# Attention scores in three matmuls per key block: three full ones before; two full ones and one over 32 rows after

## The chip, the cores and the metric

The kernel runs on one core of a Trainium2 chip. A core has five engines with a queue of instructions each: PE (TensorE, matrix products; its weight loads are listed apart as PEld), DVE (VectorE), ACT (ScalarE), POOL (GpSimd) and SP (SyncE, which here only issues DMAs). The engines run on their own and wait for each other through semaphores. Each takes its instructions in the order in which the build wrote them down. PE reads from SBUF and writes to PSUM; a bank of PSUM holds a tile of 128x512 float32 numbers in this kernel. The metric is the time of one execution on the device in microseconds (us), lower being better.

## What is computed

The program is one block of a transformer: modulated norms, an input projection, latent attention over 2048 tokens and 256 context tokens, a retention branch, an output projection and a convolutional feed-forward part. The change is in the scores of the attention:

```python
def softmax_attention(q, k, v):
    s = jnp.einsum('bqhd,bkhd->bhqk', q, k).astype(jnp.float32) * MLA_SCALE
    p = jax.nn.softmax(s, axis=-1).astype(v.dtype)
    return jnp.einsum('bhqk,bkhd->bqhd', p, v)
```

There are 8 heads. A query and a key have 96 features: 64 without position ("nope") and 32 rotary ones ("pe"; those of the key are the same for all heads). There are 2304 keys (2048 + 256).

## The kernel before

PE multiplies in float32r, so a float32 operand is kept as two float32r parts, high and low, whose sum is the operand. A product of two such operands is a sum of up to four products of parts.

**Tiles of the attention.** The outer loop runs over 128 pairs of a head and a tile of 128 queries (i = 0 to 127, 16 tiles for each head). The keys come in five blocks `CH`: four of 512 and one of 256. For each pair and block, `qk(i, ci)` makes the scores `sc` (128 queries x up to 512 keys) in one PSUM bank: three matmuls that add into the bank (L875), then one DVE instruction that scales them into the SBUF tile `p` and takes their maximum (L877). The operands are stacked along the 128 rows of the array. `ka` has the 64 nope features of the keys, the high part in rows 0 to 63 and the low part in rows 64 to 127. `kp` has the 32 rotary features as high, high, low, low. The query tile `q` (`q_first`, later `qp`) has three slabs: nope high twice, nope low twice, and rotary high, low, high, low. So each matmul fills all 128 rows, and the three of them make all four products of parts.

**What follows the scores.** `soft(i)` takes the maximum over the blocks and ACT makes the exponentials of a row of 2304 (L889). Two iterations later `tr` transposes `p` in pieces of 128x128 on PE (L914) into a PSUM tile `tr` (up to four pieces in a bank), ACT copies it as the high part `ph` (L67), and DVE makes the low part `pl` (L68). Then `pv` multiplies with the values (L929, L930). A retention branch (`ret_back`) runs in the same stage with little work.

**PSUM.** The stage uses eight banks: three for `sc` (pool `ats`), four for `tr` and one for `pv`.

**Order.** The attention loop calls its functions by a list of numbers for each i. The tile framework then orders the instructions of each engine itself at build time, by the program's order and by when it expects operands and buffers, so that instructions of neighbouring calls stand mixed. That order is fixed in the program. SP loads `ka` and `vv` one head ahead and `qp` one block of 512 queries ahead.

**Another place with a short matmul.** In the first stage, `columns` makes matmuls over 5 rows with 2 columns to stream (L278); `gemv` (L267) uses 4 columns of the array, and so does the transpose of the row sums in `inv` (L896).

Of the kernel before, what the change touches and what calls it, by code (L numbers as in the profile page):

```python
# [9 lines left out]
F32 = mybir.dt.float32  # L10
# [8 lines left out]
P = 128  # L19
# [3 lines left out]
KT = D // P  # L23
# [15 lines left out]
def hybrid_block(ctx: ExitStack, tc: tile.TileContext, x, xT, c, cx, c_ctx, w_ada1, b_ada1, w_ada2, b_ada2, g_norm1,  # L39
# [44 lines left out]
    def rms_inv(ms, n):  # L84
        """(ms + EPS) ** -0.5 for n columns"""
        r = small.tile([P, 8], F32, name="rstd")
        pool.tensor_scalar(out=r[:, :n], in0=ms, scalar1=EPS, scalar2=None, op0=ALU.add)
        pool.tensor_tensor(out=r[:, :n], in0=r[:, :n], in1=mhalf[:, :n], op=ALU.pow)
        return r
# [20 lines left out]
    # chunks of tokens of the FFN: first token, tokens, first of the tokens read (four more, one on each inner side at least)  # L110
# [10 lines left out]
    wmx = ExitStack()  # L121
    wmm = wmx.enter_context(tpool(name="wm", bufs=1))
    with ExitStack() as rf:
# [22 lines left out]
        def row_norm(src, xt, pl_, tag):  # L146
            """a token tile and the inverse of its norm"""
# [8 lines left out]
        def prep_norm(ti, pl_, tag):  # L156
            """a token tile with the features on the partitions, and the inverses of the tokens' norms in every partition"""
# [11 lines left out]
        def prep(ti):  # L169
            """normed, modulated and split"""  # L170
# [15 lines left out]
        def kv_state(first, kvs):  # L186
            """states before the first chunk, forward and backward"""
# [22 lines left out]
        # modulation of the first stage and projections of the context, by blocks of 256 features  # L210
        with tpool(name="ada", bufs=1) as ap_, tpool(name="adap", bufs=1, space=PSUM) as pp:
# [8 lines left out]
            # columns: high and low part for c, the same for c_ctx; unsplit beside zeros  # L220
# [32 lines left out]
            def gemv(b, q):  # L253
                """a quarter of the products of c and c_ctx with the weights of a block"""
# [15 lines left out]
            def columns(b):  # L270
                """shift and scale of a block, features on the partitions"""
# [91 lines left out]
        def mod_units(mp):  # L363
            """modulation of the later stages: gt1, sh2, sc2, gt2"""
# [145 lines left out]
    # 4 KB slots, shared by the raw weights of the last stages  # L510
# [16 lines left out]
    kp = kq.tile([P, NK], F32R, name="kp")  # L527
# [3 lines left out]
    def load_k(ka, h, b):  # L531
        o, n = BLK[b]
        for a in range(2):
            dma(ka[64 * a:64 * a + 64, o:o + n], kn_d[a][b][h * 64:(h + 1) * 64, :])

    def load_kp(b):
        o, n = BLK[b]
        dma(kp[:, o:o + n], kp_d[b])

    def load_q(q, h, b):  # L540
        for a in range(2):
            for r in range(2):
                dma(q[64 * r:64 * r + 64, a, :], qn_d[a][b][h * 64:(h + 1) * 64, :])
        for r in range(4):
            dma(q[32 * r:32 * r + 32, 2, :], qp_d[r % 2][b][h * 32:(h + 1) * 32, :])

# [1 line left out]
    with tpool(name="mpw", bufs=1) as wmp, tpool(name="mp", bufs=2) as wk, \  # L548
# [32 lines left out]
        def front(ti):  # L581
            """latents and rotary key of one token tile"""
# [192 lines left out]
    with tpool(name="at", bufs=2) as wk, \  # L775
            tpool(name="atp", bufs=1, space=PSUM) as pp, tpool(name="ats", bufs=3, space=PSUM) as pps:
# [15 lines left out]
        def ret_back(ti):  # L792
# [3 lines left out]
            cp = pp.tile([P, 512], F32, name="tr", bufs=4)  # L796
# [21 lines left out]
            ps = pp.tile([P, 512], F32, name="tr", bufs=4)  # L818
# [44 lines left out]
        def qk(i, ci):  # L863
# [9 lines left out]
            sc = pps.tile([P, 512], F32, name="sc")  # L873
            for a in range(3):
                pe.matmul(sc[:, 0:cn], lhsT=q[:, a, qs], rhs=(ka if a < 2 else kp)[:, c0:c0 + cn],  # L875
                          start=(a == 0), stop=(a == 2))
# [14 lines left out]
        def inv(h, b):  # L891
            """1 / row sums of a block of queries, as a row on 64 partitions"""
            rs = state.pop(("rs", h, b))
            dve.reciprocal(rs, rs)
            ps = pp.tile([P, 512], F32, name="tr", bufs=4)
# [8 lines left out]
        def tr(i, ci):  # L904
# [7 lines left out]
            ps = pp.tile([P, 512], F32, name="tr", bufs=4)  # L912
# [38 lines left out]
        def first_wo(i, k):  # L951
            """a part of the output projection's first tile, between the last products of the attention"""
# [5 lines left out]
        for i in range(NI + 3):  # L958
# [8 lines left out]
            if i >= 3 and j < NI // 2:  # L967
                if i % 2:
                    todo += [(3.7, pv, j, 0), (4.7, pv, j, 1)]
                else:  # L970
                    todo += [(0.7, pv, j, 2), (1.7, pv, j, 3), (2.7, pv, j, 4)]
# [27 lines left out]
            if i == NI - 1:  # L999
                split_wo(0, (w1, "ka1"), pool)  # L1000
                split_wo(1, (w1, "p"), pool)
                oT1 = kq.tile([P, 2, KT, P], F32R, name="oT1", tag="kp")
# [13 lines left out]
    def up_raw(f, tiles=None):  # L1016
        """weights of a pair of tiles of up-projected features (linear part, gated part), in halves of the rows"""
# [12 lines left out]
    # The up projection of a pair of tiles [2 x 128 features] x [2 x 512 rows] and of a chunk [2 x 512 rows] x  # L1030
    # [2 halves of the tokens] goes by Strassen's and Winograd's seven products of halves.
    # Operands from weights: A (linear; rows 1, 2), G (gated; rows 1, 2)
    #   S1 = G1 + G2, S2 = S1 - A1, S3 = A1 - G1, S4 = A2 - S2
    # operands from tokens: X, Y (rows 1; halves 1, 2), V, W (rows 2; halves 1, 2)
    #   T1 = Y - X, T2 = W - T1, T3 = W - Y, T4 = V - T2
    # linear: A1 X + A2 V | A1 X + S2 T2 + S1 T1 + S4 W
    # gated: A1 X + S2 T2 + S3 T3 + G2 T4 | A1 X + S2 T2 + S3 T3 + S1 T1
    WHOME = {"A1": 0, "S1": 0, "S2": 0, "S3": 0, "A2": 1, "G2": 1, "S4": 1}

    def up_w(f, *ks, home=None):  # L1040
        """operands from weights"""
# [19 lines left out]
    def up_sums(c_, k, va, vb):  # L1061
        """sums of the operands from the tokens of a chunk, for a pair of blocks of rows, in two places of memory"""
# [482 lines left out]
```

## Time and profile before

| | |
|---|---|
| median of 3 runs | 3487.3 us (3483.93 to 3490.97) |
| span of the profiled execution | 3483.1 us |
| busy in the span | PE 3301.2 us (95%), PEld 2938.8 (84%), DVE 2816.8 (81%), ACT 1657.4 (48%), POOL 1705.5 (49%) |
| attention stage, 762 to 1714 us of the span | PE 943.89 of 952 us, DVE 792.89, ACT 661.24 |
| mean granted TensorE clock | 0.984 of full speed |

How to read it: a PE row is a group of matmuls; its busy time runs from the start of the first to the modelled end of the last, and since matmuls overlap at their ends, the distance from start to start (the step) tells more than the duration. A PEld row is a weight load, which normally goes on under the matmul before it. "idle" in brackets is how long the engine stood still before the row, with what released it; "issue" means that nothing which the profile shows was waited for. The form "128*128" gives the rows and columns of the array that an instruction uses, "5*128" means 5 rows.

### The profile page before, as it was taken

What the parts mean: (1) busy time and instruction counts of PE and PEld (TensorE: products, weight loads), DVE (VectorE), ACT (ScalarE), POOL (GpSimd) and SP (SyncE); (2) the same over time, 40 slices, a digit from 0 to 9 for tenths busy, and PEclk for the clock granted to TensorE, in tenths of its full rate; (3) what the DMA queues carried; (4) which work ended last, traced back from release to release, by engine and by line L of the source; (5) the groups of instructions that cost most, each with busy time, mean ns of one, the idle gap of its engine ahead of it and who ended that gap; (6) DMA issues with size and microseconds to landing.
All of it is one profiled execution on the core that took longest, in us unless ns stands there. A gap on an engine that the chain in (4) does not pass through costs nothing. (4 is left out here: it accounts for less than half of the span.)

```text
span 3483.1 us, 53186 instructions
## 1 busy us (share of the span) xinstructions
PE 3301.2 (95%) x19262; PEld 2938.8 (84%) x19262; DVE 2816.8 (81%) x4969; ACT 1657.4 (48%) x2791; POOL 1705.5 (49%) x1440
## 2 busy tenths in 40 slices
PE   7999999999999999999999998998899998899998
PEld 4888889888999999999987887887788887788887
DVE  4666654457888888888765899999999999999998
ACT  4333334336676766776632343444444444333333
POOL 2322223222111111111144899888788887777774
PEclk9999999999999999999999999999999999999999
DMA  7444435773232232221146434223322223321212
GB/s 267 151 154 146 146 111 191 237 248 103 82 95 80 83 89 89 59 77 56 48 145 185 144 119 141 73 73 123 124 80 82 76 73 121 121 67 61 67 61 79
DMA packets 233822, 394.26 MB, mean 113 GB/s; under 512 B 29508, under 2 KB 106948, under 8 KB 233304
## 3 DMA queue, kind: packets, MB, share of 16 engines
q1 hardware_dynamic: 184640, 334.86, 30.3%
q10 hardware_dynamic: 48920, 56.01, 4.8%
q8 instruction: 152, 2.49, 0.3%
q14 instruction: 110, 0.90, 0.1%
HBM read 293.76 MB, written 97.01 MB: 112 GB/s over the span
## 5 line engine op out<-in xcount | busy, mean ns | idle before, releaser
L68 DVE TENSOR_TENSOR pl<-tr,ph 128x512 fp32r<-128x512 f32 (+1 forms) x640 | 389.1, 629 | 85.5 <-ACT ph L67 85.1
L877 DVE TENSOR_SCALAR_CACHE_REDUCE p<-sc 128x512 f32<-128x512 f32 (+1 forms) x640 | 393.0, 628 | 62.2 <-PE sc L875 50.7
L1151 PE MATMUL u<-T,wS 128*128 128x322 f32 (+1 forms) x2376 | 418.3, 323 | 8.2 <-DVE ua L1296 4.7
L67 ACT CAST ph<-tr 128x512 fp32r<-128x512 f32 (+1 forms) x640 | 329.8, 544 | 198.4 <-PE tr L914 190.5
L1151 PEld LDWEIGHTS u<-T,wS 128*128 128x128 f32 x2376 | 392.1, 191 | 27.3 <-issue 5.0
L71 PE MATMUL d<-dw,z 128*128 128x512 f32 x704 | 297.0, 422 | 113.6 <-DVE acc L1373 112.3
L875 PE MATMUL sc<-ka,qp 128*128 128x512 f32 (+1 forms) x1120 | 346.7, 391 | 0.0
L914 PE MATMUL tr<-ident,p 128*128 128x128 f32 x2304 | 343.3, 273 | 0.0
L889 ACT ACTIVATE p<-p,nb 128x2304 f32<-128x2304 f32 x128 | 284.8, 2225 | 64.3 <-DVE nb L884 60.7
L929 PE MATMUL pv<-ph,vv 128*128 128x256 f32 x1152 | 312.5, 297 | 0.0
L914 PEld LDWEIGHTS tr<-ident,p 128*128 128x128 f32 x2304 | 275.7, 140 | 33.8
L930 PE MATMUL pv<-pl,vv 128*128 128x256 f32 x1152 | 292.5, 286 | 0.0
L73 PE MATMUL d<-dw,z 128*128 128x512 f32 x704 | 283.5, 403 | 2.2 <-DVE z L68 2.2
L72 PE MATMUL d<-dw,z 128*128 128x512 f32 x704 | 284.3, 404 | 0.0
L71 PEld LDWEIGHTS d<-dw,z 128*128 128x128 f32 x704 | 135.2, 192 | 160.5 <-DVE acc L1373 139.1
L945 POOL TENSOR_TENSOR oT<-oT,rB 64x512 f32<-64x512 f32 x32 | 41.1, 1285 | 460.3 <-DVE oT L940 455.4
L68 POOL TENSOR_TENSOR wA<-ust,wA 128x512 fp32r<-128x512 f32 x130 | 208.5, 1604 | 82.9 <-ACT wA L67 82.8
L1373 DVE TENSOR_TENSOR acc<-acc,d 128x512 f32<-128x512 f32 x352 | 235.8, 677 | 15.3 <-PE d L73 13.3
L1353 POOL TENSOR_TENSOR dst<-dst,gt 128x512 f32<-128x512 f32 x132 | 237.8, 1815 | 14.4 <-DMA dst<-in_w_down_dram 11.8
L68 POOL TENSOR_TENSOR wS<-ust,wS 128x512 fp32r<-128x512 f32 x130 | 207.3, 1611 | 70.3 <-ACT wS L67 70.3
L68 POOL TENSOR_TENSOR wS<-s,wS 128x512 fp32r<-128x512 f32 x132 | 234.8, 1778 | 7.0 <-ACT wS L67 6.9
L875 PE MATMUL sc<-kp,qp 128*128 128x512 f32 x620 | 232.6, 375 | 0.0
(371 smaller groups left out, 8726.3 us busy)
## 6 DMA issues: line engine op xcount, KB each, us to landing
ust<-in_w_up_dram SPq DMA_DIRECT2D x132, 512.0 KB
dst<-in_w_down_dram SPq DMA_DIRECT2D x132, 256.0 KB
xt<-in_x_dram SPq DMA_DIRECT2D x32, 512.0 KB
wtg<-in_w_ada_dram SPq DMA_DIRECT2D x64, 256.0 KB
qp<-qn_d SPq DMA_DIRECT2D x124, 128.0 KB
v_d<-vt SPq DMA_DIRECT2D x18, 512.0 KB
wt<-in_w_ada_dram SPq DMA_DIRECT2D x16, 512.0 KB
xc<-in_xT_dram SPq DMA_DIRECT2D x16, 512.0 KB
```

What stands on the lines that cost most here:

```text
L67: act.copy(hi, src)
L68: (eng or dve).tensor_tensor(out=lo, in0=src, in1=f32(hi), op=ALU.subtract)
L71: pe.matmul(ps, lhsT=l[0], rhs=r[0], start=first, stop=False)
L72: pe.matmul(ps, lhsT=l[0], rhs=r[1], start=False, stop=False)
L73: pe.matmul(ps, lhsT=l[1], rhs=r[0], start=False, stop=last)
L875: pe.matmul(sc[:, 0:cn], lhsT=q[:, a, qs], rhs=(ka if a < 2 else kp)[:, c0:c0 + cn], start=(a == 0), stop=(a == 2))
L877: dve.tensor_scalar(out=p[:, c0:c0 + cn], in0=sc[:, 0:cn], scalar1=SCALE, scalar2=None, op0=ALU.mult, op1=ALU.max, accum_out=mx[:, ci:ci + 1])
L889: act.activation(p, p, AF.Exp, bias=nb, accum_out=state["rs", h, b][:, k:k + 1])
L914: pe.transpose(ps[:, k * P:(k + 1) * P], p[:, (k0 + k) * P:(k0 + k + 1) * P], ident)
L929: pe.matmul(o[:, 0:256], lhsT=vv[:, kk, :], rhs=ph[:, k, :], start=(kk == 0), stop=False)
L930: pe.matmul(o[:, 0:256], lhsT=vv[:, kk, :], rhs=pl[:, k, :], start=False, stop=(kk == NKT - 1))
L1151: pe.matmul(ps[:, 0:nh], lhsT=w[:, a, k, :], rhs=t[b][:, k, :], start=(k == 0 and a == b), stop=(k == HK - 1 and a == 1))
```

## The change

The three matmuls of a block are arranged anew. The first stays (nope high against key nope high and low). The second now holds, along its 128 rows, nope low against key nope high (rows 0 to 63), rotary high against key rotary high (64 to 95) and rotary high against key rotary low (96 to 127), in a new operand `kb`, of which there are two, one for even and one for odd heads. What is left, rotary low against key rotary high, is a matmul over 32 rows only: key block c lies in rows 32c to 32c + 31 of a new tile `kr`, and the third slab of the query tile has rotary low four times, once for each quarter of the rows. In the program text the 32-row matmuls of blocks 0 to 3 stand together ahead of the others, each into its own bank. The products of a low part with a low part are left out. PSUM is shared out as four banks for `sc` and three for `tr`. Three lines that time `pv` within an iteration, and the tag of a later buffer, change too.

```diff
-    kp = kq.tile([P, NK], F32R, name="kp")
+    kb = [kq.tile([P, NK], F32R, name=f"kb{a}") for a in range(2)]
+    kr = kq.tile([P, 768], F32R, name="kr")
...
         for a in range(2):
             dma(ka[64 * a:64 * a + 64, o:o + n], kn_d[a][b][h * 64:(h + 1) * 64, :])
+        dma(kb[h % 2][0:64, o:o + n], kn_d[0][b][h * 64:(h + 1) * 64, :])
...
-        dma(kp[:, o:o + n], kp_d[b])
+        for t in kb:
+            dma(t[64:96, o:o + n], kp_d[b][0:32, :])
+            dma(t[96:128, o:o + n], kp_d[b][64:96, :])
+        c, r = divmod(b, 4)
+        dma(kr[32 * r:32 * r + 32, 512 * c:512 * c + n], kp_d[b][0:32, :])
...
-        for a in range(2):
-            for r in range(2):
-                dma(q[64 * r:64 * r + 64, a, :], qn_d[a][b][h * 64:(h + 1) * 64, :])
+        for r in range(2):
+            dma(q[64 * r:64 * r + 64, 0, :], qn_d[0][b][h * 64:(h + 1) * 64, :])
+            dma(q[64 + 32 * r:96 + 32 * r, 1, :], qp_d[0][b][h * 32:(h + 1) * 32, :])
+        dma(q[0:64, 1, :], qn_d[1][b][h * 64:(h + 1) * 64, :])
         for r in range(4):
-            dma(q[32 * r:32 * r + 32, 2, :], qp_d[r % 2][b][h * 32:(h + 1) * 32, :])
+            dma(q[32 * r:32 * r + 32, 2, :], qp_d[1][b][h * 32:(h + 1) * 32, :])
...
-            tpool(name="atp", bufs=1, space=PSUM) as pp, tpool(name="ats", bufs=3, space=PSUM) as pps:
+            tpool(name="atp", bufs=1, space=PSUM) as pp, tpool(name="ats", bufs=4, space=PSUM) as pps:
...
-            cp = pp.tile([P, 512], F32, name="tr", bufs=4)
+            cp = pp.tile([P, 512], F32, name="tr", bufs=3)
...
-            sc = pps.tile([P, 512], F32, name="sc")
-            for a in range(3):
-                pe.matmul(sc[:, 0:cn], lhsT=q[:, a, qs], rhs=(ka if a < 2 else kp)[:, c0:c0 + cn],
-                          start=(a == 0), stop=(a == 2))
+            if ci in (0, 4):
+                for c in range(ci, min(ci + 4, 5)):
+                    rs, n = slice(32 * (c % 4), 32 * (c % 4) + 32), CH[c][1]
+                    state["sc", c] = pps.tile([P, 512], F32, name="sc")
+                    pe.matmul(state["sc", c][:, 0:n], lhsT=q[rs, 2, qs], rhs=kr[rs, 512 * (c // 4):512 * (c // 4) + n],
+                              start=True, stop=False)
+            sc = state.pop(("sc", ci))
+            for a in range(2):
+                pe.matmul(sc[:, 0:cn], lhsT=q[:, a, qs], rhs=(ka, kb[h % 2])[a][:, c0:c0 + cn], start=False, stop=(a == 1))
...
-                    todo += [(3.7, pv, j, 0), (4.7, pv, j, 1)]
+                    todo += [(2.7, pv, j, 0), (4.7, pv, j, 1)]
                 else:
-                    todo += [(0.7, pv, j, 2), (1.7, pv, j, 3), (2.7, pv, j, 4)]
+                    todo += [(0.7, pv, j, 2), (2.7, pv, j, 3), (4.7, pv, j, 4)]
...
-                oT1 = kq.tile([P, 2, KT, P], F32R, name="oT1", tag="kp")
+                oT1 = kq.tile([P, 2, KT, P], F32R, name="oT1", tag="kb0")
```

The build's order on PE, at two places. First, PE's first rows of the attention before the change; the numbers in the names tell buffers apart, so that one `sc` number is one key block.

```order
L875 MATMUL sc_7419<-ka_first_4835,q_first_4836 128x512 x2
L875 MATMUL sc_7419<-kp_4834,q_first_4836 128x512
L875 MATMUL sc_7424<-ka_first_4835,q_first_4836 128x512 x2
L875 MATMUL sc_7424<-kp_4834,q_first_4836 128x512
L875 MATMUL sc_7429<-ka_first_4835,q_first_4836 128x512 x2
L875 MATMUL sc_7429<-kp_4834,q_first_4836 128x512
```

The same place in the changed kernel; `kr` marks the matmuls over 32 rows (L886).

```order
L886 MATMUL sc_7447<-kr_4836,q_first_4838 128x512
L886 MATMUL sc_7449<-kr_4836,q_first_4838 128x512
L886 MATMUL sc_7451<-kr_4836,q_first_4838 128x512
L886 MATMUL sc_7453<-kr_4836,q_first_4838 128x512
L890 MATMUL sc_7447<-ka_first_4837,q_first_4838 128x512
L890 MATMUL sc_7447<-kb0_4834,q_first_4838 128x512
L890 MATMUL sc_7449<-ka_first_4837,q_first_4838 128x512
```

For the first tile of queries the four 32-row matmuls stand together, ahead of the full ones. Second, PE in the middle of the attention before the change (within head 5).

```order
L875 MATMUL sc_16041<-ka1_15206,qp_15615 128x512 x2
L875 MATMUL sc_16041<-kp_4834,qp_15615 128x512
L875 MATMUL sc_16053<-ka1_15206,qp_15615 128x512 x2
L875 MATMUL sc_16053<-kp_4834,qp_15615 128x512
L914 MATMUL tr_16046<-ident_63,p_15823 128x128 x4
L875 MATMUL sc_16065<-ka1_15206,qp_15615 128x512 x2
L875 MATMUL sc_16065<-kp_4834,qp_15615 128x512
```

A like place of the changed kernel, also within head 5; `pv` rows there belong to the tiles before.

```order
L886 MATMUL sc_15459<-kr_4836,qp_15295 128x256
L890 MATMUL sc_15459<-ka1_15273,qp_15295 128x256
L890 MATMUL sc_15459<-kb1_4835,qp_15295 128x256
L943 MATMUL pv_15345<-ph_15220,vv0_13664 128x256
L886 MATMUL sc_15495<-kr_4836,qp_15295 128x512
L890 MATMUL sc_15495<-ka1_15273,qp_15295 128x512
L890 MATMUL sc_15495<-kb1_4835,qp_15295 128x512
L886 MATMUL sc_15497<-kr_4836,qp_15295 128x512
L890 MATMUL sc_15497<-ka1_15273,qp_15295 128x512
L890 MATMUL sc_15497<-kb1_4835,qp_15295 128x512
```

Here each 32-row matmul stands alone, right ahead of the two full ones of its own block. In PE's whole order the four stand together once, at the first tile; the other 636 of the 640 stand alone, each with full matmuls or transposes on both sides.

## Rows read from the trace of the kernel before

**Rows 1.** Busy us (and instructions) of PE, PEld, DVE, ACT, POOL; clock; DMA.
```profile
762.00:1714.00 952.00, 943.89 (x6652) 863.16 (x6652) 792.89 (x2320) 661.24 (x1035) 168.45 (x140) 0.99 0.28 82
```

**Rows 2.** Waits of PE in the attention: us in total, times, longest.
```profile
PE sc L875 <- DVE p L877: 8.1, 1, 8.1
```

**Rows 3.** Groups of instructions in the attention: busy us, mean ns, idle before.
```profile
L877 DVE TENSOR_SCALAR_CACHE_REDUCE p<-sc 128x512 f32<-128x512 f32 x511 | 342.1, 682 | 52.9 <-PE sc L875 42.3 <-PE tr L914 6.3
...
L68 DVE TENSOR_TENSOR pl<-tr,ph 128x512 fp32r<-128x512 f32 x503 | 336.5, 683 | 81.7 <-ACT ph L67 81.4
...
L889 ACT ACTIVATE p<-p,nb 128x2304 f32<-128x2304 f32 x127 | 282.5, 2225 | 64.3 <-DVE nb L884 60.7 <-DVE pl L68 1.5 <-DVE p L877 1.0
L67 ACT CAST ph<-tr 128x512 fp32r<-128x512 f32 x504 | 281.5, 586 | 155.0 <-PE tr L914 147.5 <-DVE pl L68 6.2
```

**Rows 4.** Timeline of PE on one key block: start us, us, engine, line.
```profile
1506.41 0.39 PE L875 MATMUL sc<-kp,qp 128*128 128x512 f32 x1
...
1506.64 0.63 PE L875 MATMUL sc<-ka,qp 128*128 128x512 f32 x2
...
1507.10 0.39 PE L875 MATMUL sc<-kp,qp 128*128 128x512 f32 x1
```

**Rows 5.** Timeline where PE goes from full matmuls to 5-row ones.
```profile
32.56 0.57 ACT L275 COPY rows<-pr 4x512 f32<-4x512 f32 x1
...
36.69 0.19 PEld L73 LDWEIGHTS po<-wr,hx 128*128 128x128 f32 x1
...
36.92 0.39 PE L73 MATMUL po<-wr,hx 128*128 128x512 f32 x1
...
37.24 0.18 PEld L278 LDWEIGHTS tr<-rcol,rows 5*128 5x128 f32 x1 [0.36 <-issue]
37.24 0.27 PE L278 MATMUL tr<-rcol,rows 5*128 5x2 f32 x1
```

**Rows 6.** Timeline where PE goes from transposes to 5-row matmuls.
```profile
23.30 0.66 PE L238 MATMUL tr<-ident,xc 128*128 128x128 f32 x4
...
23.89 0.29 PEld L278 LDWEIGHTS tr<-rcol,rows 5*128 5x128 f32 x2 [0.17 <-issue]
```

**Rows 7.** Timeline where PE goes back from 5-row matmuls to full ones.
```profile
54.37 0.61 ACT L67 CAST hx<-hf 128x512 fp32r<-128x512 f32 x1
...
54.52 1.05 PE L278 MATMUL tr<-rcol,rows 5*128 5x2 f32 x8 [1.12 <-ACT rows L275]
...
55.49 0.19 PEld L71 LDWEIGHTS po<-wr,hx 128*128 128x128 f32 x1
55.49 0.50 PE L71 MATMUL po<-wr,hx 128*128 128x512 f32 x1
55.83 0.40 PE L72 MATMUL po<-wr,hx 128*128 128x512 f32 x1
```

**Rows 8.** Timeline where PE uses 4 columns between full matmuls.
```profile
35.05 0.39 PE L72 MATMUL po<-wr,hx 128*128 128x512 f32 x1
...
35.28 0.63 PE L267 MATMUL pr<-wt,s 128*4 128x512 f32 x2
...
35.75 0.40 PE L73 MATMUL po<-wr,hx 128*128 128x512 f32 x1
...
1498.03 0.28 PE L930 MATMUL pv<-pl,vv 128*128 128x256 f32 x1
...
1498.05 0.08 PEld L896 LDWEIGHTS tr<-ident,rs 128*4 128x4 f32 x1
...
1498.15 0.19 PEld L929 LDWEIGHTS pv<-ph,vv 128*128 128x128 f32 x1
```

**Rows 9.** Timeline of SP: a query block's nope loads as they are issued.
```profile
1509.45 2.38 SPq L58 DMA_DIRECT2D qp<-qn_d x4
```

More of the change, by code (lines that the diff above doesn't have):

```diff
@@ L817, in ret_back @@
             yield
-            ps = pp.tile([P, 512], F32, name="tr", bufs=4)
+            ps = pp.tile([P, 512], F32, name="tr", bufs=3)
             for h in range(RH):
@@ L894, in inv @@
             dve.reciprocal(rs, rs)
-            ps = pp.tile([P, 512], F32, name="tr", bufs=4)
+            ps = pp.tile([P, 512], F32, name="tr", bufs=3)
             pe.transpose(ps[0:QN, 0:P], rs, ident)
@@ L911, in tr @@
             p = state["p", i]
-            ps = pp.tile([P, 512], F32, name="tr", bufs=4)
+            ps = pp.tile([P, 512], F32, name="tr", bufs=3)
             for k in range(kn):
```

## The prediction

> **What bounds the kernel now.** I began with the busy times by stretches. In the attention stage PE is busy 943.89 of 952.00 us at a granted clock of 0.99, while DVE has 792.89 us of work and ACT 661.24 [rows 1]. The 8.1 us that PE lacks are one single wait [rows 2]; everywhere else in the stage its next instruction could start. So the stage lasts as long as PE's work: 952 / 128 = 7.44 us for each tile of 128 queries. DVE's idle time there is time in which it waits for PE's scores or for ACT's copy of the transposes [rows 3], so DVE is the next bound, 17% below PE. What the change is worth is therefore read from the steps of PE. In a key block, matmuls over 128 rows and 512 columns follow each other every 0.23 us: 1506.41, 1506.64, and after two of them 1507.10 [rows 4]. Each lasts 0.39 us, so a matmul's end lies 0.39 - 0.23 = 0.16 us after the last of its columns went in.
>
> **The change part by part.**
>
> *The matmuls themselves.* Before, a block of 512 keys takes three steps of 0.23 us. After, it takes two full matmuls and one over 32 rows that streams the same 512 columns. Only if the four 32-row matmuls run side by side do their columns cost less. For that they have to stand next to each other in PE's order, and by the order that the build wrote down they do so once, at the first tile. The other 636 stand alone, each ahead of the two full matmuls of its own block. The reason can be read from the order too: a 32-row matmul opens a bank, the banks of `sc` come free one at a time as DVE empties them, and when one comes free PE is given that block whole. So the columns saved are those of one tile, 3 x 0.23 = 0.7 us in all, which I neglect. Columns cost as much as before.
>
> *Going to 32 rows and back.* This is the term that decides. No row of before has a float32r matmul over 32 rows. The nearest ones are the float32 matmuls over 5 rows in the first stage, of which I take the three places where nothing else was waited for.
> On the way in: a weight load normally starts with the matmul before it, as that of L73 does at 36.69 [rows 5]. L73 itself starts at 36.92, and its columns are through one step later, at 37.15. The load for five rows starts only at 37.24, 0.09 us after that, with PEld idle for no cause that the profile shows; its data had been copied since 33.13 (32.56 + 0.57) [rows 5]. The two-column matmul ends at 37.51; less the 0.16 us, its columns go in at 37.35. That is 0.43 us after those of L73, where a step is 0.23: 0.20 us lost. After transposes it is alike: the four end at 23.96, and the load of the five-row matmuls starts at 23.89 after 0.17 us of idle time put down to issue [rows 6].
> On the way out: the eight five-row matmuls end at 55.57 (54.52 + 1.05), so the columns of the last go in at about 55.41, and being two they need next to no time. The load for L71 starts at 55.49, though its operand was cast by 54.98; L71 ends at 55.99, so its columns go in at 55.99 - 0.39 = 55.60 [rows 7]. That is 0.19 us lost; the next matmul comes one step on, its end at 56.23.
> So a visit to 32 rows would cost 0.20 + 0.19 = 0.39 us, for 512 and for 256 columns alike, since it is made of the end of one matmul and the load for the next. There are 636 + 1 = 637 visits: 637 x 0.39 = 248 us.
> Bounds of this term: below, nothing. Float32r matmuls that use 4 columns of the array come and go without a gap: 35.05, 35.28, two steps, 35.75; a transpose with 4 columns between `pv` matmuls has its load at once as well, at 1498.05 and 1498.15 [rows 8]. These change columns, not rows. If only the late start of the load counts and the load itself is hidden, 0.09 us twice: 115 us. I take the 5-row rows, since they are the only ones that change the number of rows, and they show the gap each time.
> The Trainium skill, page "TensorEngine Tiling (Array Packing)", section Tiling Modes (Key Properties), says that going from one tiling mode to another drains TensorE, and counts 128x32 as a mode like 32x128. The five-row rows agree (0.09 us from the last column to the next load); the 4-column rows do not, and there the measurement decides. By the page every visit drains twice, and the time is the one of the sum below; by rows of the 4-column kind none does, and it is that of the first rival.
>
> *Banks.* Four for `sc` instead of three, three for `tr` instead of four. A bank of `tr` is held from the transposes through ACT's copy (0.59 us) and DVE's subtraction (0.68), and up to one exponential of 2.23 us on ACT and some DVE work may lie ahead [rows 3]: some 2 to 4.5 us. Three banks come round every 3/5 of a tile, 4.5 us at the old pace and 3/5 x (7.44 + 5 x 0.39) = 5.6 at the new one. With the lost time in place this is covered; without it, a few tenths of a microsecond in a tile may show. I take nothing, with an upper bound of 0.3 us a tile, 38 us. DVE and ACT work as before and have more room, not less: 6.2 and 5.2 us in 9.4.
>
> *Loads.* `kb` adds 5 loads for each of 8 heads, `kp` becomes 20 more, a query block has 9 for 8 (32 more): 92, at 2.38 / 4 = 0.6 us each on SP 55 us of issuing [rows 9], spread over the attention and the stage before it. `kb` of a head is loaded during the head before, and the queue stands idle more than it works; DMA is busy 28% there [rows 1]. What it costs if that cover is gone: the last block's loads before the first tile, 5 x 0.6 = 3 us, once. I take nothing.
>
> **The sum.** 3483.1 us (span) + 248 = 3731 us. The median of the runs is 4.2 us above the span, so 3735 us is what I expect of it. The attention stage would go from 952 to 1200 us, 9.4 us a tile; the stages before and after keep their order (after the attention, eight lines of PE's order differ) and so their times.
>
> **The rivals.**
> *Float32r over 32 rows comes and goes without a gap.* The 4-column rows speak for it: there a change of shape costs nothing [rows 8]. Against it: those keep all rows. Then PE's steps are as before, and the time is 3487 us, up to 3525 if three banks for `tr` show.
> *Half the price:* the load is hidden behind the gap (115 us, 3602), or only one of the two ways costs (0.2 x 637 = 127 us, 3615).
> *The four run side by side after all* and the kernel is faster. Per tile the full three matmuls over 4.5 blocks are 13.5 steps, 3.1 us; two full ones are 9 steps, and the quarters one of 512 and one of 256 columns, 1.5 steps: 3 steps less, 0.69 us, 88 us in all, 3399 us. DVE would allow it: 793 us of work in 864. It is decided by the order alone: it needs the four next to each other in most tiles, and they are so in one of 128. I can see only a PE that overlaps a 32-row matmul with neighbours that fill all rows, for which no row speaks.
> The Trainium skill, page "TensorE: Matmul & The Clock Gate", Part 3, gives 3.07 times for four 32-row matmuls of 512 columns in different row groups; at that figure (an estimate) four would take 4 x 0.23 / 3.07 = 0.30 us. No row here shows four together.
>
> **How the numbers follow.** Full price 0.74, half price 0.10, no gap 0.12, side by side 0.03, more than 38 us above the sum 0.01. The predicted time is that of the full price; its own range is 3700 to 3775 (0.34 to 0.39 us a visit, and the banks' 38 us). The range for 8 in 10 takes in the half price: 3595 to 3775. A measurement of this kernel can tell about 0.2%, 7 us, from no change. Faster: side by side, and 0.02 of the no-gap case, 0.05. Same: 0.07 of the no-gap case. Slower: the rest, 0.88.
>
> **What would show it.** In the profile after: weight loads of L886 that start some 0.32 us after the full matmul ahead of them instead of with it, and those of the first L890 likewise after the 32-row matmul; each block some 1.08 us of PE instead of 0.69 us; 9.4 us a tile; DVE waiting for `sc` more than before; no wait of PE for DVE beyond single ones. If L886's loads start with the matmul ahead, the main term is wrong. If PE's waits for `tr` or `sc` banks grow, the bank term is; and if the granted clock of the stage falls below 0.99 with PE no longer full, a cost that I left out has come in.

## The result and the profile after

The changed kernel takes 3769.9 us (median of 4 runs, 3758.59 to 3783.52) against 3485.7 us in the same series: 1.0815 times, 95% interval 1.0789 to 1.0841. It is slower by 284 us, and the time lies in the predicted range, 35 us above its point. The span of its profiled execution is 3769.6 us.

Nearly all of it came in the attention. From its first `sc` matmul to its last `pv` matmul it took 973.3 us before (762.4 to 1735.7) and 1252.6 us after (764.9 to 2017.4), 279 us more; the stage ahead is 2.4 us longer and the rest 4.8 us. The windows (busy us and instructions of PE, PEld, DVE, ACT, POOL; clock; DMA) show it in the time span of [rows 1], in a stretch of its middle and in one near its end.

```profile
762.00:1714.00 952.00, 942.93 (x5205) 687.64 (x5206) 627.40 (x1839) 514.99 (x816) 146.36 (x128) 0.99 0.26 77
1000.00:1200.00 200.00, 198.57 (x1117) 145.39 (x1115) 131.90 (x385) 109.80 (x172) 24.70 (x23) 1.00 0.21 64
1800.00:2000.00 200.00, 194.86 (x1014) 141.28 (x1013) 120.30 (x337) 101.00 (x155) 18.22 (x10) 0.94 0.11 33
```

Against [rows 1], PE is as busy as before (942.93 of 952 us) but gets through 5205 matmuls in place of 6652. DVE and ACT fall with it, so neither is the bound. PE is slower at its own work, which a busy time can't show; its steps can. The timelines of PE and of its weight loads on two key blocks of the same tile:

```profile
1508.79 0.50 PE L886 MATMUL sc<-kr,qp 32*128 32x512 f32 x1
1509.22 0.50 PE L890 MATMUL sc<-ka,qp 128*128 128x512 f32 x1
1509.55 0.40 PE L890 MATMUL sc<-kb,qp 128*128 128x512 f32 x1
1509.88 0.50 PE L886 MATMUL sc<-kr,qp 32*128 32x512 f32 x1
...
1509.22 0.19 PEld L890 LDWEIGHTS sc<-ka,qp 128*128 128x128 f32 x1 [0.24 <-issue]
1509.32 0.19 PEld L890 LDWEIGHTS sc<-kb,qp 128*128 128x128 f32 x1
1509.88 0.18 PEld L886 LDWEIGHTS sc<-kr,qp 32*128 32x128 f32 x1 [0.37 <-issue]
```

A block takes 1.09 us (1508.79 to 1509.88) where [rows 4] has 0.69. The load for the 32-row matmul starts at 1509.88, 0.33 us after the full matmul of 1509.55, and the load for the next full one only 0.43 us after the 32-row matmul; the load of `kb`, between two full matmuls, starts at 1509.32, with 0.23 us to go. These are the two gaps of [rows 5] and [rows 7], in float32r and at 32 rows.

Two things are new. The waits of PE in the attention (us in total, times, longest) hold short waits for `sc` in 29 places, where [rows 2] had a single one of 8.1 us, which is gone:

```profile
PE sc L886 <- DVE p L891: 12.3, 29, 0.8
PE tr L928 <- DVE pl L68: 1.9, 4, 0.6
```

And the granted clock falls to the lower of its two levels, 1.2 GHz, for 47.8 us of the stage in five stretches (before: 10.2 us in one). The first begins at 1302.9. The timeline of PE there has a wait for a bank, lone 32-row matmuls, and then a full matmul of 0.79 us for 0.50:

```profile
1299.43 0.38 PE L928 MATMUL tr<-ident,p 128*128 128x128 f32 x2
1300.61 0.38 PE L886 MATMUL sc<-kr,qp 32*128 32x256 f32 x1 [0.79 <-DVE p L891]
...
1301.35 0.49 PE L886 MATMUL sc<-kr,qp 32*128 32x512 f32 x1
...
1302.43 0.49 PE L886 MATMUL sc<-kr,qp 32*128 32x512 f32 x1
1302.85 0.79 PE L890 MATMUL sc<-ka,qp 128*128 128x512 f32 x1
```

**PE's steps, added up.** For every two neighbouring matmuls of the stage I took the distance between their ends, less what such a matmul takes in an unbroken row (0.233 us for 512 columns, 0.119 for 256, 0.109 for a transpose), and added these excesses by kind. They sum to 288.7 us after and 10.5 before; the difference, 278, is the stage's 279 but for 1 us (8.7 of the 10.5 before are the one long wait of [rows 2]). At full clock 624 steps into 32 rows lose 134.3 us and 622 out of them 122.5; the rest is 27 such steps at the lower clock (12.5 us) and 19 us of other steps, most of them transposes and at the lower clock too. At 0.39 us the 637 visits are 248 us of the difference; some 30 us more are to be explained.

### The profile page after: what moved, and what is told of

It is laid out like the page before. It is cut to its first block, busy times and chain, and to the rows that moved or that the text cites. A ratio compares the mean times of both kernels' runs of the same rounds, so it can differ in the third digit from the quotient of the medians.

```text
span 3769.6 us, 53343 instructions
## 1 busy us (share of the span) xinstructions
PE 3575.0 (95%) x19262; PEld 2959.3 (79%) x19262; DVE 2831.6 (75%) x4969; ACT 1653.9 (44%) x2791; POOL 1705.9 (45%) x1440
## 4 chain that ended last, share of the span: by engine, by line
PE 60%; DVE 23%; issue 6%; POOL 4%; DMA 4%; ACT 2%; SPq 0%; DVEq 0%; ACTq 0%; POOLq 0%
PE sc L890 11%; PE sc L886 7%; PE tr L928 7%; PE u L1165 6%; PE pv L943 4%; PE pv L944 4%; PE pj L71 3%; PE pj L72 3%; PE pj L73 3%; DVE s L1067 2%; DVE acc L1387 2%; DVE ya L1287 2%; DVE th L1349 2%; PE d L71 2%; DVE z L68 1%
## 5 line engine op out<-in xcount | busy, mean ns | idle before, releaser
L891 DVE TENSOR_SCALAR_CACHE_REDUCE p<-sc 128x512 f32<-128x512 f32 (+1 forms) x640 | 377.7, 631 | 111.5 <-PE tr L928 105.7
L944 PE MATMUL pv<-pl,vv 128*128 128x256 f32 x1152 | 316.1, 305 | 0.3 <-DVE pl L68 0.3
L886 PE MATMUL sc<-kr,qp 32*128 32x512 f32 x620 | 295.4, 476 | 12.0 <-DVE p L891 12.0
L943 PE MATMUL pv<-ph,vv 128*128 128x256 f32 x1152 | 303.9, 289 | 0.0
L890 PE MATMUL sc<-ka,qp 128*128 128x512 f32 (+1 forms) x560 | 271.3, 485 | 0.0
```

Of the source, the lines that this page charges most:

```text
L886: pe.matmul(state["sc", c][:, 0:n], lhsT=q[rs, 2, qs], rhs=kr[rs, 512 * (c // 4):512 * (c // 4) + n], start=True, stop=False)
L890: pe.matmul(sc[:, 0:cn], lhsT=q[:, a, qs], rhs=(ka, kb[h % 2])[a][:, c0:c0 + cn], start=False, stop=(a == 1))
L891: dve.tensor_scalar(out=p[:, c0:c0 + cn], in0=sc[:, 0:cn], scalar1=SCALE, scalar2=None, op0=ALU.mult, op1=ALU.max, accum_out=mx[:, ci:ci + 1])
L943: pe.matmul(o[:, 0:256], lhsT=vv[:, kk, :], rhs=ph[:, k, :], start=(kk == 0), stop=False)
L944: pe.matmul(o[:, 0:256], lhsT=vv[:, kk, :], rhs=pl[:, k, :], start=False, stop=(kk == NKT - 1))
```

## The experiments

Two theories. **Visits:** each visit of PE to 32 rows has one price, 0.39 us. **Banks, order, loads:** the loss, or part of it, comes from four banks for `sc` and three for `tr` in place of three and four, from the rotary matmuls written ahead of their blocks, or from the new loads. All runs compute what the changed kernel computes; those that read more rows than hold data have zeros in the others. The table gathers them; "four ahead" means that the program text has the rotary matmuls of blocks 0 to 3 ahead of the others, as in the changed kernel; "stage" is from the first `sc` matmul to the last `pv` matmul of the profiled execution.

| run | visits | banks sc/tr | median us | ratio to before, 95% | stage us |
|---|---|---|---|---|---|
| before | 0 | 3/4 | 3484.6 to 3487.1 | 1 | 973.3 |
| e9 | 0 | 3/4 | 3493.2 | 1.0019 (1.0010 to 1.0028) | 979.6 |
| e8 | 256 | 3/4 | 3585.0 | 1.0287 (1.0271 to 1.0303) | 1071.3 |
| e2 | 640 | 3/4 | 3736.4 | 1.0712 (1.0689 to 1.0735) | 1222.2 |
| e10 (64 rows) | 640 | 3/4 | 3729.5 | 1.0697 (1.0682 to 1.0712) | 1212.1 |
| e11 | 0 | 3/3 | 3570.6 | 1.0248 (1.0231 to 1.0266) | 1061.9 |
| e5 | 0 | 4/3 | 3583.9 | 1.0284 (1.0267 to 1.0301) | 1072.2 |
| e1 (four ahead) | 0 | 4/3 | 3587.2 | 1.0290 (1.0273 to 1.0308) | 1074.4 |
| e4 (four ahead) | 256 | 4/3 | 3642.6 | 1.0450 (1.0434 to 1.0465) | 1127.4 |
| after (four ahead) | 637 | 4/3 | 3769.9 | 1.0815 (1.0789 to 1.0841) | 1252.6 |
| e12 | 640 | 4/3 | 3773.5 | 1.0823 (1.0801 to 1.0844) | 1279.4 |
| e3 (four together) | 128 | 4 as one/3 | 3879.7 | 1.1132 (1.1114 to 1.1149) | 1371.7 |
| e6 (four together) | 128 | 4/3 | 3581.9 | 1.0279 (1.0263 to 1.0294) | 1073.2 |
| e7 (three together) | 128 | 3/4 | 3528.4 | 1.0125 (1.0109 to 1.0140) | 1016.3 |

### e1: all rows

```diff
-    kr = kq.tile([P, 768], F32R, name="kr")
+    kr = kq.tile([P, NK], F32R, name="kr")
+    pool.memset(f32(kr), 0.0)
...
-                    pe.matmul(state["sc", c][:, 0:n], lhsT=q[rs, 2, qs], rhs=kr[rs, 512 * (c // 4):512 * (c // 4) + n],
+                    pe.matmul(state["sc", c][:, 0:n], lhsT=q[:, 2, qs], rhs=kr[:, CH[c][0]:CH[c][0] + n],
```

> The changed kernel with one thing undone: the matmul over the rotary keys reads all 128 rows, with zeros under its 32 rows, so its numbers are the same and it never goes to 32 rows; the order of the program's code and the banks (four for the scores, three for the transposes) stay as changed. If the visits to 32 rows are the loss (0.39 us each, 637 of them, 248 us), the time falls from 3770 to 3485 to 3525 us: 3770 less 248 is 3522, and less if the waits and the stretches at the lower clock go with the visits. If the banks, the order of the code or the four-fold loads of queries are the loss, it stays above 3700 us.

Measured: 3587.2 us, what neither theory gave. The visits are gone and 183 us with them, but 100 us are left, with PE waiting for banks (lines at e5).

### e2: visits with the banks of before

```diff
-            tpool(name="atp", bufs=1, space=PSUM) as pp, tpool(name="ats", bufs=4, space=PSUM) as pps:
+            tpool(name="atp", bufs=1, space=PSUM) as pp, tpool(name="ats", bufs=3, space=PSUM) as pps:
...
-            cp = pp.tile([P, 512], F32, name="tr", bufs=3)
+            cp = pp.tile([P, 512], F32, name="tr", bufs=4)
...
+            r, g = ci % 4, 512 * (ci // 4)
+            sc = pps.tile([P, 512], F32, name="sc")
+            pe.matmul(sc[:, 0:cn], lhsT=q[32 * r:32 * r + 32, 2, qs], rhs=kr[32 * r:32 * r + 32, g:g + cn],
+                      start=True, stop=False)
```

> The changed kernel with its 32-row matmuls kept, but each is written with its own block again, and the scores have three banks and the transposes four, as before the change. If the visits to 32 rows are the loss, it stays at 3735 to 3775 us (3735 if the waits for banks and the lower clock came from the banks, 3770 if they come from the visits). If banks and order are the loss, it falls to 3500 us or less.

Measured: 3736.4 us. In its windows PE is full and the clock is whole, so nothing but PE's own steps is left:

```profile
1000.00:1200.00 200.00, 200.00 (x1128) 148.83 (x1126) 139.39 (x396) 112.50 (x177) 24.77 (x24) 1.00 0.22 63
1800.00:1980.00 180.00, 180.00 (x1015) 134.74 (x1015) 120.39 (x324) 102.46 (x156) 23.08 (x12) 1.00 0.13 36
```

Its steps at full clock: 626 into 32 rows lose 0.192 us each on average, 619 out into a score matmul 0.197. That is 0.39 us a visit, the price of the prediction.

### e4: two blocks of five

```diff
+                    rs = slice(32 * c, 32 * c + 32) if c in (0, 2) else slice(0, P)
...
-                    pe.matmul(state["sc", c][:, 0:n], lhsT=q[rs, 2, qs], rhs=kr[rs, 512 * (c // 4):512 * (c // 4) + n],
+                    pe.matmul(state["sc", c][:, 0:n], lhsT=q[rs, 2, qs], rhs=kr[rs, CH[c][0]:CH[c][0] + n],
```

> As the run with full rows, but blocks 0 and 2 of each query tile go to 32 rows and blocks 1, 3 and 4 read all 128 rows with zeros: 256 visits in place of 637. If each visit has its price (0.39 us), the time is that of the run with full rows plus 100 us, 3585 to 3625 us. If the price is by tile, paid once however many visits a tile has, it stays within 30 us of the changed kernel's 3770 us.

Measured: 3642.6 us, 55 us above e1 and outside both expectations. Its steps say why: the visits lose 102 us at full clock (253 in, 0.207 each, and 254 out, 0.196), but the losses of the other `sc` and `tr` steps, 39.0 and 60.6 us in e1, are 23.6 and 26.6 here. A PE that visits comes later to the banks, and waits less for them.

### e3: four together in one tile of four banks

```diff
+            if ci == 0:
+                state["sc"] = pps.tile([P, 4, 512], F32, name="sc")
+                for c in range(4):
+                    rs = slice(32 * c, 32 * c + 32)
+                    pe.matmul(state["sc"][:, c, :], lhsT=q[rs, 2, qs], rhs=kr[rs, :], start=True, stop=False)
+            if ci < 4:
+                sc = state["sc"][:, ci, :]
+            else:
+                sc = pp.tile([P, 512], F32, name="tr", bufs=3)
+                pe.matmul(sc[:, 0:cn], lhsT=q[:, 2, qs], rhs=k4, start=True, stop=False)
```

> The four 32-row matmuls of blocks 0 to 3 are made to stand together at every query tile: the four blocks' scores are one tile of four banks, so that all four become ready at once; block 4's rotary part reads all 128 rows with zeros, into a bank of the transposes. If a visit has one price and the four run side by side, a tile takes 0.30 us less on PE than before the change (four rotary parts at 0.93 us become one at 0.24 and one visit at 0.39): 128 times 0.30 is 38 us, 3448 us, unless the one four-bank tile makes PE wait for the evictions, which could cost up to 1 us per tile (3490 to 3600 us) with PE waiting at the 32-row matmuls' line for DVE. If the four don't run side by side, 0.70 us per tile more: 3537 us with no such wait in the trace.

Measured: 3879.7 us, the slowest of all and above every expectation, although the four stand together at all 128 tiles and run side by side. First the timeline of PE, then its waits in the attention:

```profile
1510.25 0.50 PE L890 MATMUL sc<-kr,qp 32*128 32x512 f32 x4
1510.68 0.51 PE L897 MATMUL sc<-ka,qp 128*128 128x512 f32 x1
```

```profile
PE sc L897 <- DVE p L898: 105.3, 109, 6.8
PE sc L890 <- DVE p L898: 63.6, 76, 1.1
```

Four take the 0.43 us that one takes in the changed kernel. The waits, as I read them, are of this way to write it: all four banks are one tile, so the full matmuls of one bank (L897) wait until DVE has emptied the bank before it, and the next tile's four (L890) until all are empty. With PE standing still so often, 300 us of the stage run at the lower clock (mean of the execution 0.949). It shows the four side by side and says nothing of what that is worth.

### e5: each rotary matmul with its own block again

```diff
-            if ci in (0, 4):
-                for c in range(ci, min(ci + 4, 5)):
...
-            sc = state.pop(("sc", ci))
+            sc = pps.tile([P, 512], F32, name="sc")
+            pe.matmul(sc[:, 0:cn], lhsT=q[:, 2, qs], rhs=kr[:, c0:c0 + cn], start=True, stop=False)
```

(against the changed kernel, with the full rows of e1)

> The run with full rows (3587 us, 100 us over before although it makes no visit to 32 rows) with one more thing undone: each block's rotary matmul is written with its own block again; the scores keep four banks and the transposes three. If the 100 us come from the transposes' third bank less, it stays at 3570 to 3600 us. If they come from the four rotary matmuls that take their banks ahead of their blocks, it falls to 3480 to 3500 us.

Measured: 3583.9 us, as e1. The order of the code is not it. A window of e5, its waits in the attention, and PE's timeline (only transposes):

```profile
1000.00:1200.00 200.00, 194.47 (x1299) 167.97 (x1298) 152.90 (x460) 127.00 (x203) 32.51 (x32) 1.00 0.29 89
```

```profile
PE tr L924 <- DVE pl L68: 12.1, 48, 0.8
PE sc L884 <- DVE p L887: 11.8, 39, 0.8
```

```profile
1007.10 1.04 PE L924 MATMUL tr<-ident,p 128*128 128x128 f32 x8
...
1008.92 0.60 PE L924 MATMUL tr<-ident,p 128*128 128x128 f32 x4
...
1010.71 1.04 PE L924 MATMUL tr<-ident,p 128*128 128x128 f32 x6
1011.91 0.66 PE L924 MATMUL tr<-ident,p 128*128 128x128 f32 x4 [0.16 <-DVE pl L68]
```

PE lacks 5.5 of 200 us, though the columns are those of before. The waits list only what exceeds a matmul's modelled end (24 us in these rows); by the steps, transposes lose 58.5 us at full clock and score matmuls 39.5, where before they lost 0.9 and 8.2 (nearly all of it the one long wait). The row at 1011.91 shows such a wait: after 18 transposes in 4.6 us, which take five banks in turn (up to four go into one, and there are three), the next waits until DVE has made the low part of an earlier one and its bank is free. Why the banks come free late, the timelines of ACT and DVE show:

```profile
1007.15 2.22 ACT L899 ACTIVATE p<-p,nb 128x2304 f32<-128x2304 f32 x1
...
1009.36 1.54 ACT L67 CAST ph<-tr 128x512 fp32r<-128x512 f32 x3
```

```profile
1009.96 1.89 DVE L68 TENSOR_TENSOR pl<-tr,ph 128x512 fp32r<-128x512 f32 x3 [2.85 <-ACT ph L67]
```

The first twelve transposes fill all three banks while ACT is at an exponential. Its copies begin only after that, at 1009.36, and DVE, for which PE waits by name, has itself stood idle 2.85 us for them. It is so all over the stage: 124 of the 640 groups of transposes start within 0.1 us of DVE's release of the bank three groups back. Such a bank was held 3.3 us on average; 1.4 of them (169 us in all) lie between its transposes and ACT's copy, and for 145 of these 169 us ACT was at an exponential.

### e6: four together, separate banks, the 32 rows last

```diff
             for a in range(2):
-                pe.matmul(sc[:, 0:cn], lhsT=q[:, a, qs], rhs=(ka, kb[h % 2])[a][:, c0:c0 + cn], start=False, stop=(a == 1))
+                ins = pe.matmul(sc[:, 0:cn], lhsT=q[:, a, qs], rhs=(ka, kb[h % 2])[a][:, c0:c0 + cn], start=(a == 0), stop=False)
+            if ci < 4:
+                state["sc", ci] = sc
+                if ci < 3:
+                    return
+                with tc.issue_after(ins.ins):
+                    for c in range(4):
+                        rs = slice(32 * c, 32 * c + 32)
+                        pe.matmul(state["sc", c], lhsT=q[rs, 2, qs], rhs=kr[rs, 512 * c:512 * c + 512], start=False, stop=True)
```

(DVE's four evictions follow; `issue_after` only fixes PE's order)

> The four 32-row matmuls stand together at every query tile, as in the run with one tile of four banks, but the four score banks stay separate tiles and the 32-row matmuls come last: the two full matmuls of blocks 0 to 3 first, then the four together; block 4 reads all rows with zeros; four banks for the scores, three for the transposes. If a visit has one price whatever stands in it and the four share one matmul's time, PE has 0.30 us less per tile than before the change: 3448 us where nothing else waits. If three banks for the transposes cost what the run with full rows shows (100 us), it comes to about 3550 us, with PE waiting for banks. If the four don't share their time in this place, 89 us more than either.

Measured: 3581.9 us, 2 us under e5, which has the same banks and no visits, and 32 over the 3550 expected with waits. The timeline of PE and its loads, a window, and a wait in the attention:

```profile
1500.85 0.40 PE L885 MATMUL sc<-kb,qp 128*128 128x512 f32 x1
1501.18 0.50 PE L893 MATMUL sc<-kr,qp 32*128 32x512 f32 x4
1501.61 0.38 PE L951 MATMUL pv<-ph,vv 128*128 128x256 f32 x1
...
1501.18 0.19 PEld L893 LDWEIGHTS sc<-kr,qp 32*128 32x128 f32 x4 [0.36 <-issue]
```

```profile
1000.00:1200.00 200.00, 187.99 (x1297) 151.21 (x1296) 152.99 (x451) 128.25 (x206) 32.25 (x30) 1.00 0.30 88
```

```profile
PE tr L936 <- DVE pl L68: 30.8, 60, 0.7
```

The theory of the visits holds on PE. At full clock 130 steps in lose 25.1 us (0.193 each), the steps out 27.4, and 382 steps from one quarter to the next save 88.1 (0.231 each, all but 0.002 us of a step): 36 us less, as expected. But the waits grow by as much: transposes lose 85.3 us and score matmuls 49.2, 37 us more than in e5 (of the score matmuls' 49.2, 13.1 are one step with a long wait near the stage's start). PE has less to do and stands still longer (187.99 of 200 us busy); it is no longer the bound.

### e7: three together with the banks of before

```diff
-            if ci < 4:
+            if ci < 3:
...
-            tpool(name="atp", bufs=1, space=PSUM) as pp, tpool(name="ats", bufs=4, space=PSUM) as pps:
+            tpool(name="atp", bufs=1, space=PSUM) as pp, tpool(name="ats", bufs=3, space=PSUM) as pps:
...
-            ps = pp.tile([P, 512], F32, name="tr", bufs=3)
+            ps = pp.tile([P, 512], F32, name="tr", bufs=4)
```

(against e6; blocks 3 and 4 read all rows)

> The same with three together (blocks 0 to 2; blocks 3 and 4 read all rows with zeros) and the banks as before the change, three for the scores and four for the transposes. On PE: three rotary parts at 0.233 us become one and a visit at 0.39, 0.075 us less per tile, 10 us in all: 3477 us where nothing else waits. If the blocks that are now finished together make VectorE come late and PE wait for banks, 3500 to 3600 us, with those waits in the trace.

Measured: 3528.4 us, 35 us over e9. On PE the visits (24.5 us in, 33.4 out, of which 8.4 are one step with a long wait) and the steps saved (59.0) cancel. Score matmuls lose 34.0 us and transposes 15.2, against 11.1 and 1.6 in e9. PE's waits in the attention name DVE's evictions (in e9 they did so 3 times, for 9.8 us, 9.2 of them in one):

```profile
PE sc L885 <- DVE p L899: 17.2, 39, 1.0
```

That three banks are held until all three blocks are done, and then wait for DVE together, fits this and the edit; no run took it away alone.

### e9: neither visits nor banks

```diff
-            tpool(name="atp", bufs=1, space=PSUM) as pp, tpool(name="ats", bufs=4, space=PSUM) as pps:
+            tpool(name="atp", bufs=1, space=PSUM) as pp, tpool(name="ats", bufs=3, space=PSUM) as pps:
...
-            ps = pp.tile([P, 512], F32, name="tr", bufs=3)
+            ps = pp.tile([P, 512], F32, name="tr", bufs=4)
```

(against e5)

> No visit to 32 rows (all 128 rows, zeros under the 32), each rotary matmul with its own block, and the banks as before the change: three for the scores, four for the transposes. What is left of the change is the contents of the operands, the loads and one more fill with zeros. If these cost nothing, the time is that of before, 3480 to 3495 us. If a part of the 100 us of the two runs with full rows came from them and not from the banks, it stays above 3500 us.

Measured: 3493.2 us, 1.0019 (1.0010 to 1.0028). All the rest of the change, loads, contents and the new places of `pv`, costs 6.6 us. Some 4 of them are waits, most near the stage's start (PE waits 12.1 us in the attention, against the 8.1 of [rows 2]); the rest no row accounts for.

### e8: 256 visits with the banks of before

```diff
+            rs = slice(32 * ci, 32 * ci + 32) if ci in (0, 2) else slice(0, P)
-            pe.matmul(sc[:, 0:cn], lhsT=q[:, 2, qs], rhs=kr[:, c0:c0 + cn], start=True, stop=False)
+            pe.matmul(sc[:, 0:cn], lhsT=q[rs, 2, qs], rhs=kr[rs, c0:c0 + cn], start=True, stop=False)
```

(against e9)

> As the run just above (own order, banks as before), but blocks 0 and 2 go to 32 rows: 256 visits. If a visit costs 0.39 us wherever PE has no idle time to hide it, the time is 3487 plus 100, 3575 to 3600 us. If the price per visit is what the two runs at the changed banks differ by (55 us for 256, 0.21 us), it is 3542 us, and the 249 us of the run with 640 visits at the banks of before would not be proportional to their number.

Measured: 3585.0 us, 92 us over e9: 0.36 us a visit; e2 lies 243 us over e9, 0.38 a visit. Steps in lose 0.193 us here too, steps out 0.196. The price is by visit, and proportional where PE is full. By the time of the whole program it comes out a little under the 0.39 us of the steps. One reason is that waits go where visits come: PE's 12.1 us of waits in the attention of e9 are 6.6 in e8 and none in e2.

### e10: 64 rows

```diff
+            rs = slice(64 * (ci % 2), 64 * (ci % 2) + 64)
+            pe.matmul(sc[:, 0:cn], lhsT=q[rs, 2, qs], rhs=kr[rs, c0:c0 + cn], start=True, stop=False)
```

> As the run with no visits, but each rotary matmul reads 64 rows (32 of keys, 32 of zeros) in place of 128: 640 visits to 64 rows, none to 32. If the price is for any step between matmuls of 128 rows and of fewer, it is as with 32 rows, 3725 to 3745 us. If only 32 rows have it, 3480 to 3495 us; if it grows with the rows that are left idle, in between.

Measured: 3729.5 us, 236 us over e9, 0.37 a visit. The timeline has the same late steps (0.31 us from `kr` to `ka` at 256 columns, where a step is 0.12):

```profile
1500.28 0.36 PE L940 MATMUL pv<-ph,vv 128*128 128x256 f32 x1
1500.57 0.38 PE L885 MATMUL sc<-kr,qp 64*128 64x256 f32 x1
1500.88 0.39 PE L887 MATMUL sc<-ka,qp 128*128 128x256 f32 x1
1501.10 0.28 PE L887 MATMUL sc<-kb,qp 128*128 128x256 f32 x1
```

### e12 and e11: which of it the banks are

e12, against the changed kernel, writes each 32-row matmul with its own block, as e2 does, and keeps the changed banks. e11, against e5:

```diff
-            tpool(name="atp", bufs=1, space=PSUM) as pp, tpool(name="ats", bufs=4, space=PSUM) as pps:
+            tpool(name="atp", bufs=1, space=PSUM) as pp, tpool(name="ats", bufs=3, space=PSUM) as pps:
```

> The changed kernel with one thing undone: each 32-row matmul is written with its own block, not four ahead; four banks for the scores and three for the transposes as changed. It tells what the 34 us are that the changed kernel takes over the run with its visits but the banks of before (3736 us). If they are the banks', it stays at 3760 to 3780 us; if they are the order's, it falls to 3728 to 3745 us.

> No visits, own order, as the run at 3584 us with four banks for the scores and three for the transposes, but three and three, with one bank of eight left empty. If the 91 us over the run with three and four come from the transposes' fourth bank, it stays at 3580 to 3600 us, or more if the scores' fourth bank gave something back; if they come from a fourth bank for the scores (it lets the build write another order), it falls to 3485 to 3500 us.

Measured: 3773.5 us for e12 (its profiled execution is longer than that, 3784.8 us, with 105.8 us of the stage at the lower clock), so the changed kernel's excess over e2 is the banks' and not the order's. 3570.6 us for e11: with three and three, 77 of the 91 us between e9 and e5 are there already. It is the fourth bank of `tr` that is missed; the fourth of `sc` brings nothing here, and costs 13 us more; why it costs is not shown.

## Why the prediction was right, and what it left out

**That PE's steps bound the stage** was right: in e2 PE is busy 200.00 of 200.00 us, and the time follows its steps. (The 952 us taken for the stage leave out its last 22; the sum does not use them.)

**Columns cost as before, and 637 visits** was right. The first tile shows what was not costed, because it happens once: four side by side, in the time of one.

```profile
764.89 0.51 PE L886 MATMUL sc<-kr,q_first 32*128 32x512 f32 x4
765.33 0.50 PE L890 MATMUL sc<-ka_first,q_first 128*128 128x512 f32 x1
```

**0.39 us a visit, from the 5-row float32 matmuls,** was right to the second digit: 0.20 + 0.19 predicted, 0.192 + 0.197 in e2, and alike for 512 and 256 columns, as argued (in e2 0.192 and 0.191 in, 0.197 out for both). Without the banks the sum of 3735 us meets e2's 3736. That it does so to 1 us is in part luck: e2 loses some 10 us more in 24 us at the lower clock at the stage's start, and lacks the wait of 8.1 us of [rows 2]. The rival of no gap and those of half the price are out: no run has 0.2 us a visit where PE is full. The Trainium skill, page "TensorEngine Tiling (Array Packing)", section Tiling Modes, says that a change of mode drains TensorE; the runs agree for 32 rows (e2) and for 64 (e10), at 0.19 to 0.20 us each way. Over 128 rows and 4 columns there is no gap: in e9 such a transpose starts at 1501.17 and the next `pv` matmul at 1501.19. The prediction took this to be against the page; but the page does not say that a matmul of 4 columns runs in its 128x32 mode, and no run shows it.

**Banks taken as nothing** is the step that failed. The visits alone cost 249 us (e2), the banks alone 100 (e1) and both together 284, not 349. In the changed kernel the cover, the time lost in visits, was there as argued, but it did not take all: 34 us over e2 were left where the sum has nothing, within the upper bound of 38. Two signs of error that the prediction named came with it: more waits for `sc`, and a granted clock under 0.99 (0.94 from 1800 to 2000). With that cover gone the banks cost 91 to 100 us, not the 38 that the bound allowed.

The bound came from average times: 4.5 us for three banks to come round against 2 to 4.5 us that one is held. The averages were about right; in e5 three groups of transposes come round in 5.0 us on average, and a bank is held for 3.6. But the 124 starts that follow a release at once stand where three groups came in 3.4 us. And in the kernel before, where an average of 4.5 us against 2.9 would have left room, a group of transposes started in 69 of 640 cases with the bank three groups back still held: it went into the fourth. So it is the bursts, with ACT's exponential ahead of the copies, that need the fourth bank; no run spread the transposes out or moved the exponential. The first rival would have ended near 3587 us, not at 3487 to 3525.

**Where the 34 us went in the changed kernel.** Its steps exceed those of e2 by 30.4 us, as its stage does (1252.6 less 1222.2). Steps into 32 rows lose 14.4 us more (134.3 for 119.9), which are the waits for `sc`; transposes at full clock 4.6 more; and the steps at the lower clock some 11 more. The fall of the clock goes with visits and long waits together. Five of the 29 waits for `sc` last 0.79 us, the others 0.36 at most; the wait at 1300.61 is the first of the five, and each of the five falls begins 0.9 to 3.4 us after the end of one of them, none after the others. e12 is alike: five waits of 0.79 us, each with a fall behind it, and one fall elsewhere. After the first 65 us of the stage, the runs with visits and without such waits (e2, e8, e10 and e7) have no fall. Those without visits (e1, e5, e11) have there seven stops of PE of 0.74 us or more each, and one fall of 3.4 us between them. But e4 (256 visits) has seven such stops and one fall of 10.2 us, and e6 (128 visits) sixteen and one of 3.4, so the two together don't bring a fall each time. No run took the five waits alone away from the changed kernel.

**Side by side and faster** (0.03) was wrong in its price. It is not decided by the order alone: e6 has the order and 36 us less on PE, and is no faster than e5, because the wait for banks, held until ACT has copied and DVE has emptied them, takes over. "DVE would allow it" was read from its busy time, 793 of 864 us, and did not count where its work falls. On the price of the four, the Trainium skill, page "TensorE: Matmul & The Clock Gate", Part 3, has 3.07 times for four 32-row matmuls of 512 columns; in e6 each of the three further ones adds 0.002 us to a step of 0.233, close to four times; but the visit's 0.39 us comes on top, which leaves 0.63 us for the four against 0.93 for four full steps.

No version here beats the kernel before.

## What to carry to other kernels

Count the changes of row shape, not the rows: between streams of 128-row matmuls in float32r one short matmul cost its columns and 0.39 us, wherever PE was the bound. So a remainder over 32 rows is better filled up with zeros, unless three or more of 512 columns stand next to each other in the order that the build writes (three save 0.47 us of columns for one visit's 0.39), and even then e6 and e7 gained nothing, since PE waited for banks instead. Reshaping work on the engine that bounds also changes how many banks the rest has; try the banks alone, since a loss there can hide under a slower engine and come out when the other is mended. Whether banks suffice is decided by the bursts and by what the emptying engine does first, not by average times. Losses of two edits don't add when one gives the time that the other waits for.

## What the runs showed of the hardware

Matmuls over 64 rows cost as much to come and go as those over 32 (0.37 and 0.38 us a visit over e9), in spite of half the array in use. Four 32-row matmuls in four quarters, into four banks, go in within the step of one: 0.43 us from the first to the load of what follows, as for one alone.
